# Layer 0's mixing half fed with x before its norm's row factor, in a two-layer hybrid decoder trunk

## The chip, the cores and the metric

The kernel runs on one core of one Trainium2 chip. The metric is the device time of one execution in microseconds (us), the median of several runs.

## The reference

Two layers, each a token-mixing half and an MLP half, over 256 tokens of 1024 channels. All arithmetic is float32.

```python
h = rmsnorm(x, ln_mix_pre[l])                 # x * rsqrt(mean(x^2) + eps) * gain
xr, yr, q, kv, g_nsa, qm, g_merge = split(h @ w_in[l])
o_a = rglru_branch(xr, yr, ...)               # conv, gates, scan, * gelu(yr)
o_b = nsa_branch(q, kv, g_nsa, positions, ...)  # rotary; compressed, selected, windowed
o_c = memory_branch(qm, mem, ln_mem[l], w_mem_kv[l])  # 4 heads into rmsnorm(mem)
merged = ga*(o_a @ w_br_rnn[l]) + gb*(o_b @ w_br_nsa[l]) + gc*(o_c @ w_br_mem[l])
x = x + rmsnorm(merged @ w_out[l], ln_mix_post[l])
x = x + rmsnorm(square(relu(rmsnorm(x, ln_mlp_pre[l]) @ mlp_w1[l])) @ mlp_w2[l], ln_mlp_post[l])
```

The row factor of a norm is one number per token, rsqrt(mean(x^2) + eps). A product h @ w is the row factor times (x * gain) @ w.

## The kernel before

Weights come from HBM in units of 128x1024 float32 (`raw`, five buffers, 512 KB each), and each unit is split into two fp32r parts: ScalarE (ACT) copies it to `whi`, and VectorE (DVE) writes the rest, `wlo` = raw - whi (`split_unit`; four buffers of each). Activations are split in the same way (`hTh` and `hTl` for layer 0's input, `hmh` and `hml` for the MLP's, `mTh` and `mTl` for the normed memory). Each product is then three matmuls: high by high, high by low, low by high. A unit is 24 matmuls of 256 columns or 12 of 512.

`ORDER0` and `ORDER1` list the jobs of each layer; `run` issues their units one after the other on TensorE (PE). In layer 0 the first job is `xr1`, the second `xr0`, then `yr0`, `yr1`, `vm0`, `km0`. All else (norms, evacuations of PSUM, scores, softmax, scans) are generators called lanes. A lane says on which engine its next piece runs, and `side`, called after each step of six or twelve matmuls, advances every lane whose next piece is due. What is due is decided by a clock per engine (`Order.T`), which `Meter` advances by a cost for every instruction as it is written; a PE piece of a lane is put in when its inputs are due at the PE's clock (`TOL` 0.07 us). So the costs in `Meter` set the order of the program, and all engines run that order as written. All instructions are recorded through line 140, so a row is told by its tiles.

The program's start: x comes as four tiles `xt[t][h]` (two of tokens by two of channels, 256 KB each). `first_norm` squares and sums them on ACT (`junk`), makes the row factor on GpSimd (POOL: `mean`, `var`, `rstd`), scales x on DVE (`hn`), and `quarter` transposes `hn` on PE (`tr`), four quarters of 256 channels, whose results are multiplied by the gain's column `gcol` as they are split. `warm` matmuls are filler, with no use of their result. The memory's norm (`mem_prep`, `mnorm`) loads six tiles (1.5 MB, gain and `mem`), squares on ACT, scales on DVE (`hn` again) and transposes on PE (`tr` again); its result is first used by `vm0`. At the end of a mixing half the residual and the MLP's norm follow in the same way (POOL `rstd`, DVE `hn`, PE `tr`).

Of the kernel before, what the change touches and what calls it, by code (L numbers as in the profile page):

```python
# [11 lines left out]
F32 = mybir.dt.float32  # L12
# [93 lines left out]
class Meter:  # L106
# [39 lines left out]
def trunk_kernel(ctx, tc, x, mem, positions, ln_mix_pre, w_in, conv_w, conv_b, lru_wr, lru_br, lru_wi, lru_bi,  # L146
# [269 lines left out]
    warm, gcol = [], []  # L416

# [16 lines left out]
    def first_norm(o):  # L434

        hn = {}

        def scale(t):
            yield "A"
            el, box = first_half(xt[t][0])  # L440
            s1 = half_sumsq(xt[t][1])
            yield el
            yield "G"
            r = rstd_of(box[0], s1)
            for h in range(2):
                yield "D"
                hn[t, h] = a([P, 512], F32, "hn")
                dve.tensor_scalar(hn[t, h], xt[t][h], r, None, op0=OP.mult)

        def quarter(q):  # L450
            while len(hn) < NT * 2 and not all((t, q // 2) in hn for t in range(NT)):
                yield scaled
# [21 lines left out]
        scaled = [spawn(scale(t), prio=0) for t in range(NT)]  # L474
        for q in range(4):
            spawn(quarter(q), f"first{q}", prio=0)

# [168 lines left out]
    def run(jobs):  # L646
# [83 lines left out]
    nsin = cp.tile([P, 3, 32], F32, name="nsin")  # L730
    per = a([P, 2, 64], F32, name="per")
# [13 lines left out]
    def rope_tables():  # L745
# [38 lines left out]
        dve.tensor_scalar(cos, h, -2.0, 1.0, op0=OP.mult, op1=OP.add)  # L784

    def rope_mul(src, nh, s, t1, t2, rows=P):

        r = slice(0, rows)
# [155 lines left out]
    def mem_score_lane(t, qm, km, pr):  # L944
# [12 lines left out]
        dve.tensor_scalar(mx, mx, -1.0 / 16, None, op0=OP.mult)  # L957
# [3 lines left out]
        for h in range(2):  # L961
            act.activation(p[:, h, :], sc[:, h, :], AF.Exp, scale=1.0 / 16, bias=mx[:, h:h + 1],
# [36 lines left out]
    def mem_lane(l, rnd, qm, km, vm, o):  # L999
        pr = {}  # L1000
        yield [spawn(mem_score_lane(t, qm, km, pr)) for t in range(NT)]
# [342 lines left out]
    def layer(l):  # L1344
# [4 lines left out]


        def xr_epi(half):
            def go(banks):
                E["xs", half] = [a([P, 2, S], F32, "xs") for _ in range(2)]
                yield "A"
                for b in range(2):
                    act.activation(E["xs", half][b], banks[b], AF.Copy)
# [3 lines left out]
        def yr_epi(half):  # L1360
            def go(banks):
                ys = [a([P, 2, S], F32, "ys") for _ in range(2)]
                yield "A"
                for b in range(2):
                    act.activation(ys[b], banks[b], AF.Copy)
# [55 lines left out]
        def g_done(half, i):  # L1421
            def lane(t, o):
                tg = E["tg", i, half, t] = a([P, 512], F32, "tg")
                yield "A"
                act.activation(tg, o, AF.Tanh, scale=0.5)
# [55 lines left out]
        def kc_epi(j, banks):  # L1481
            st = a([P, 2, S], F32, "kcs")
            yield "A"
            act.activation(st, banks[j], AF.Copy)
# [13 lines left out]
        def kv_epi(br):  # L1498
            def go(t, banks):
# [3 lines left out]
                for w in range(2):  # L1503
                    act.activation(vx[w][:, :, 0:3:2, :], dup(v[:, 2 * w:2 * w + 2], [P, 2, 2, 64]), AF.Copy)
                yield "D"
                t1, t2 = a([P, 256], F32, "rt1"), a([P, 256], F32, "rt2")
                rope_mul(banks[t][:, 0:256], 4, t, t1, t2)
                for w in range(2):
                    dve.tensor_tensor(vx[w][:, :, 1, :], v[:, 2 * w:2 * w + 2], f(vx[w][:, :, 0, :]), op=OP.subtract)
# [17 lines left out]
        def gn_job():  # L1527
# [11 lines left out]
            def lane():  # L1539
                th = a([48, S], F32, "gth")  # L1540
                yield "A"
                act.activation(th, st["b"], AF.Tanh, scale=0.5)
                free("mm")
# [14 lines left out]
        def q_epi(half):  # L1558
            def one(t, banks):
                t1, t2 = a([P, 512], F32, "rt1"), a([P, 512], F32, "rt2")  # L1560
                yield "D"
                rope_mul(banks[t], 8, t, t1, t2)
# [190 lines left out]
    def mem_prep(l):  # L1753
# [10 lines left out]
        od.cur.r = max(od.cur.r, dma_clock[0] + 2.0)  # L1764
        spawn(norm_both(ms, gm, env[l]["M"], f"mnorm{l}"))

    def load_x(t):
        for h in range(2):
# [5 lines left out]
    dma_clock[0] = 2.4 + 4 * 0.73  # L1774
# [16 lines left out]
    od.cur.r = 4.5  # L1791
    spawn(column, "gcol", prio=0)
    first_norm(env[0]["X"])
    first_pre = order[0].pre

    def start():
        first_pre()
        mem_prep(0)
# [7 lines left out]
    order[0].pre = start  # L1806
    od.cur.r = 0.0
    run(order)
# [31 lines left out]
```

## Time and profile before

| | before |
|---|---|
| median of the runs shown (1216.6 to 1221.95) | 1221.04 us |
| the profiled execution's own time | 1221.59 us |
| its span in the trace | 1219.9 us |
| PE busy | 1199.6 us of the span |
| DVE busy | 901.6 us |
| ACT busy | 736.7 us |

The span is the profiled execution from the first to the last instruction; 1.69 us of its own time lie outside. Busy time of PE is modelled with the latency of each matmul (283 ns for one of 256 columns that starts 120 ns after the one before), so short gaps don't show in it: gaps are read from the starts of matmuls in the timeline.

### The profile page before, as it was taken

The page shows a single profiled execution, that of the slowest core. Times are in us where ns is not written, and L with a number is a line of the kernel's source. Part 1 is how long each engine was busy: PE and PEld are TensorE (multiplying, and loading weights), DVE is VectorE, ACT ScalarE, POOL GpSimd, SP SyncE. Part 2 cuts the span into 40 slices and gives each one's busy share as a digit, 9 for nine tenths or more (in the row PEclk, how much of TensorE's full clock was granted, in tenths as well). Part 3 has the DMA queues.
Part 4 walks back from the last instruction along what each step waited for, and adds up shares of the span by engine and source line. Part 5 has one row for each costly group of instructions (what it writes and reads, how often), then busy time and mean ns, then how long its engine had stood idle before and what let it go on. Part 6 is the DMA issues. An engine that isn't in the chain of part 4 may idle for free.

```text
span 1219.9 us, 19570 instructions
## 1 busy us (share of the span) xinstructions
PE 1199.6 (98%) x7371; PEld 1068.8 (88%) x7371; DVE 901.6 (74%) x1516; ACT 736.7 (60%) x1330; POOL 35.5 (3%) x88
## 2 busy tenths in 40 slices
PE   8899999999999999999999999999999999999997
PEld 7899988888888889998989999888888887899896
DVE  4778897979898686555557587998978877655555
ACT  4677856777666465445456688675656655645443
POOL 3000000000000020000001000000000001000000
PEclk9899999999999999999999999999999999999999
DMA  8555656753345666666656556584534356565561
GB/s 283 181 161 168 190 156 181 223 152 108 122 131 186 233 191 191 194 189 189 206 174 210 154 171 176 153 258 140 154 121 138 121 164 217 166 187 183 190 190 69
DMA packets 121263, 212.58 MB, mean 174 GB/s; under 512 B 10441, under 2 KB 24098, under 8 KB 121169
## 3 DMA queue, kind: packets, MB, share of 16 engines
q1 hardware_dynamic: 120752, 211.19, 55.9%
q8 instruction: 58, 0.95, 0.3%
q0 software_dynamic: 416, 0.15, 0.1%
q14 instruction: 37, 0.30, 0.1%
HBM read 208.16 MB, written 1.05 MB: 172 GB/s over the span
## 4 chain that ended last, share of the span: by engine, by line
PE 92%; DVE 2%; DMA 2%; ACT 2%; issue 1%; SPq 0%; POOL 0%; POOLq 0%; DVEq 0%; ACTq 0%
PE mm L140 62%; PE acc L140 14%; PE ob L140 2%; PE sc L140 2%; PE wo L140 2%; PE pt L140 2%; PE hid L140 1%; PE gp L140 1%; PE mo L140 1%; PE msc L140 1%; PE tr L140 1%; DMA mem<-in_mem_dram 1%; ACT junk L140 1%; DVE wlo L140 1%; DMA raw<-in_mlp_w_dram 1%
## 5 line engine op out<-in xcount | busy, mean ns | idle before, releaser
L140 DVE TENSOR_TENSOR wlo<-raw,whi 128x1024 fp32r<-128x1024 f32 (+1 forms) x371 | 447.1, 1214 | 225.7 <-ACT whi L140 224.3
L140 ACT ACTIVATE whi<-raw 128x1024 fp32r<-128x1024 f32 (+1 forms) x371 | 385.3, 1055 | 204.9 <-PE mm L140 117.0
L140 PE MATMUL mm<-hmh,whi 128*128 128x256 f32 x480 | 135.9, 283 | 0.0
L140 PE MATMUL mm<-hmh,wlo 128*128 128x256 f32 x480 | 135.9, 283 | 0.0
L140 PE MATMUL mm<-hml,whi 128*128 128x256 f32 x480 | 135.9, 283 | 0.0
L140 PE MATMUL mm<-hTh,whi 128*128 128x256 f32 x448 | 129.4, 289 | 0.0
L140 PE MATMUL mm<-whi,hTh 128*128 128x512 f32 x320 | 129.1, 403 | 0.0
L140 PE MATMUL mm<-hTh,wlo 128*128 128x256 f32 x448 | 127.6, 285 | 0.0
L140 PE MATMUL mm<-hTl,whi 128*128 128x256 f32 x448 | 127.6, 285 | 0.0
L140 PE MATMUL mm<-wlo,hTh 128*128 128x512 f32 x320 | 125.1, 391 | 0.0
L140 PE MATMUL mm<-whi,hTl 128*128 128x512 f32 x320 | 125.0, 391 | 0.0
L140 PE MATMUL acc<-whi,rh 128*128 128x512 f32 x256 | 99.8, 390 | 0.0
L140 PE MATMUL acc<-wlo,rh 128*128 128x512 f32 x256 | 99.8, 390 | 0.0
L140 PE MATMUL acc<-whi,rl 128*128 128x512 f32 x256 | 99.6, 389 | 0.0
L140 PEld LDWEIGHTS mm<-hmh,whi 128*128 128x128 f32 x480 | 92.1, 192 | 0.5
L140 PEld LDWEIGHTS mm<-hml,whi 128*128 128x128 f32 x480 | 92.1, 192 | 0.5
L140 PEld LDWEIGHTS mm<-hmh,wlo 128*128 128x128 f32 x480 | 92.1, 192 | 0.0
L140 PEld LDWEIGHTS mm<-hTh,whi 128*128 128x128 f32 x448 | 86.9, 194 | 0.2
L140 PEld LDWEIGHTS mm<-hTl,whi 128*128 128x128 f32 x448 | 86.9, 194 | 0.2
L140 PEld LDWEIGHTS mm<-hTh,wlo 128*128 128x128 f32 x448 | 86.7, 194 | 0.0
L140 PEld LDWEIGHTS mm<-whi,hTl 128*128 128x128 f32 x320 | 60.1, 188 | 13.1
L140 PEld LDWEIGHTS mm<-whi,hTh 128*128 128x128 f32 x320 | 60.2, 188 | 12.0 <-issue 0.2
(311 smaller groups left out, 2467.7 us busy)
## 6 DMA issues: line engine op xcount, KB each, us to landing
raw<-in_w_in_dram SPq DMA_DIRECT2D x136, 512.0 KB, 3.7
raw<-in_mlp_w_dram SPq DMA_DIRECT2D x128, 512.0 KB, 4.2
raw<-in_w_mem_kv_dram SPq DMA_DIRECT2D x32, 512.0 KB, 4.2
raw<-in_cmp_w_dram SPq DMA_DIRECT2D x16, 512.0 KB, 4.0
raw<-in_w_br_rnn_dram SPq DMA_DIRECT2D x16, 512.0 KB, 3.7
raw<-in_w_br_mem_dram SPq DMA_DIRECT2D x16, 512.0 KB, 3.7
raw<-in_w_br_nsa_dram SPq DMA_DIRECT2D x16, 512.0 KB, 3.7
raw<-in_w_out_dram SPq DMA_DIRECT2D x16, 512.0 KB, 4.5
```

The source lines that it names most:

```text
L140: return fn(*args, **kw)
```

## The change

In layer 0's mixing half the matmuls take x times the gain, without the row factor. `quarter` transposes `xt` itself. The sums of squares, POOL's chain and the factor (`rfac`: times 1, 1/2, 1/16 and -1/16) come later, and the factor enters where a result leaves PSUM: as the scale of ACT's activation where tokens lie on partitions (merge gates, values, memory scores), in rotary tables made for layer 0 (`rot`: 6 small DVE instructions), and where tokens lie along a row, by multiplying with `rows`, the factor of all 256 tokens on every partition. `rows` is made on PE as ones times a diagonal matrix (`spread`, tile `rs`, two float32 matmuls) and copied by DVE. With `by_rows` ten 128x512 evacuations of layer 0 (4 `xs`, 4 `ys`, 2 `kcs`) move from ACT to DVE, and the branch gates' tile gets one DVE instruction more. The half of x with channels 512 to 1023 is loaded behind the first two weight units; the memory's loads and norm go from the first job to the second. In `Meter` the cost of an fp32r matmul of n columns goes from 0.0025 + n/2400 to 0.0133 + n/2400 us.

```diff
-                    cost = max(load, 0.0025 + n / 2400.0) * (4 if args[1].dtype == F32 else 1)
+                    cost = (max(load, 0.0133 + n / 2400.0) if args[1].dtype != F32 else 4 * max(load, 0.001 + n / 2400.0))
...
+    rows = cp.tile([P, S], F32, name="rows")
+    rfac = cp.tile([P, NT, 4], F32, name="rfac")
...
-    def first_norm(o):
+    def first_operands(o):
+        ones = a([P, P], F32, "ones")
+        pool.memset(ones, 1.0)
+        diag = {}
...
-                    pe.transpose(pt[:, i, t * P:(t + 1) * P], hn[t, q // 2][:, c * P:(c + 1) * P], ident)
+                    pe.transpose(pt[:, i, t * P:(t + 1) * P], xt[t][q // 2][:, c * P:(c + 1) * P], ident)
...
+        def scale(t):
+            yield "A"
+            el, box = first_half(xt[t][0])
+            s1 = half_sumsq(xt[t][1])
+            yield el
+            yield "G"
+            r = rstd_of(box[0], s1)
+            yield "D"
+            for i, c in enumerate((1.0, 0.5, 1.0 / 16, -1.0 / 16)):
+                dve.tensor_scalar(rfac[:, t, i:i + 1], r, c, None, op0=OP.mult)
+            diag[t] = a([P, P], F32, "diag")
+            dve.tensor_scalar(diag[t], ident, r, None, op0=OP.mult)
+        def spread():
+            yield [spawn(scale(t)) for t in range(NT)]
+            yield "M1"
+            pt = bank([P, NT, P], "mm", "rs")
+            for t in range(NT):
+                pe.matmul(pt[:, t, :], ones, diag[t], start=True, stop=True)
+            yield "D"
+            dve.tensor_copy(rows, pt.rearrange("p t c -> p (t c)"))
+            free("mm")
...
+    def by_rows(dst, src, shape):
+        dve.tensor_tensor(dst, src, bc(rows[:shape[0]], "p (o s) -> p o s", shape), op=OP.mult)
...
+            if nd == 2:
+                between()
...
+        def channel_copy(dst, banks):
+            if l == 0:
+                yield "@rows"
+                yield "D"
+                for b in range(2):
+                    by_rows(dst[b], banks[b], [P, 2, S])
...
-    def load_x(t):
-        for h in range(2):
+    def load_x(h):
+        dma_clock[0] += 2 * 0.73
+        for t in range(NT):
             nc.sync.dma_start(out=xt[t][h], in_=x[0, t * P:(t + 1) * P, 512 * h:512 * h + 512])
+    column = load_column(ln_mix_pre[0:1, :])
     load_x(0)
-    column = load_column(ln_mix_pre[0:1, :])
-    load_x(1)
...
     def start():
         first_pre()
-        mem_prep(0)
...
+    def second():
+        second_pre()
+        mem_prep(0)
...
+    order[0].pre, order[1].pre = start, second
+    order[2].pre = lambda: drain("rows")
+    order[11].pre = lambda: drain("const")
...
+    run(order, lambda: load_x(1))
```

How the order moves is shown at three places. The first is PE at the program's start, up to the first matmul of `xr1` (`hn` is scaled x, `xt` is x as loaded, 93 and 95 its first half of channels), before:

```order
L140 MATMUL warm_130<-dmask,identr 128x256 x16
L140 MATMUL gcol_147<-ident,grow_108 128x8
L140 MATMUL tr_183<-ident,hn_169 128x128 x2
L140 MATMUL tr_183<-ident,hn_179 128x128 x2
L140 MATMUL warm_130<-dmask,identr 128x256 x2
L140 MATMUL tr_192<-ident,hn_169 128x128 x2
L140 MATMUL tr_192<-ident,hn_179 128x128 x2
L140 MATMUL warm_130<-dmask,identr 128x256 x2
L140 MATMUL tr_199<-ident,hn_173 128x128 x2
L140 MATMUL tr_199<-ident,hn_181 128x128 x2
L140 MATMUL warm_130<-dmask,identr 128x256 x2
L140 MATMUL mm_263<-hTh_112,whi_208 128x256
```

and now:

```order
L140 MATMUL warm_136<-dmask,identr 128x256 x16
L140 MATMUL gcol_153<-ident,grow_108 128x8
L140 MATMUL tr_157<-ident,xt_93 128x128 x2
L140 MATMUL tr_157<-ident,xt_95 128x128 x2
L140 MATMUL warm_136<-dmask,identr 128x256 x2
L140 MATMUL tr_166<-ident,xt_93 128x128 x2
L140 MATMUL tr_166<-ident,xt_95 128x128 x2
L140 MATMUL warm_136<-dmask,identr 128x256 x2
L140 MATMUL mm_210<-hTh_114,whi_175 128x256
```

Three of the four quarters stood ahead of the first `mm`, and half of their transposes read tiles of either half of x; now two quarters stand ahead of it, both of the first half, and the other two follow after 12 matmuls.

The second is ACT from the splits of the fifth and sixth unit on (`junk` from `mem` is the memory's sum of squares, `xs` the evacuation of `xr1`), before:

```order
L140 ACTIVATE whi_344<-raw_128 128x1024
L140 ACTIVATE whi_374<-raw_214 128x1024
L140 ACTIVATE junk_392,ss_393<-mem_230 128x512
L140 ACTIVATE junk_395,ss_396<-mem_232 128x512
L140 ACTIVATE junk_398,ss_399<-mem_234 128x512
L140 ACTIVATE junk_401,ss_402<-mem_236 128x512
L140 ACTIVATE xs_416<-mm_263 128x512
L140 ACTIVATE xs_417<-mm_264 128x512
L140 ACTIVATE whi_426<-raw_220 128x1024
```

and now, later in the program (`whi_588` is the eleventh unit, `whi_680` the thirteenth):

```order
L140 ACTIVATE whi_588<-raw_368 128x1024
L140 ACTIVATE whi_645<-raw_403 128x1024
L140 ACTIVATE whi_680<-raw_464 128x1024
L140 ACTIVATE junk_700,ss_701<-mem_413 128x512
L140 ACTIVATE junk_703,ss_704<-mem_415 128x512
L140 ACTIVATE junk_706,ss_707<-mem_417 128x512
L140 ACTIVATE junk_709,ss_710<-mem_419 128x512
L140 ACTIVATE whi_734<-raw_530 128x1024
```

The memory's four sums stood behind the sixth unit's split and ahead of the seventh's; now they stand behind the thirteenth's and ahead of the fourteenth's, and `xs` is no longer on ACT.

The third is PE at the end of layer 0's mixing half, where the MLP's norm is transposed (`mm` is a unit of layer 1's `vm0`; `hn` the MLP's normed input, 5138 and 5140 or 5148 and 5150 the first 128 tokens), before:

```order
L140 MATMUL mm_5062<-whi_5088,mTh_4325 128x512
L140 MATMUL mm_5062<-wlo_5089,mTh_4325 128x512
L140 MATMUL mm_5062<-whi_5088,mTl_4326 128x512
L140 MATMUL mm_5063<-whi_5088,mTh_4325 128x512
L140 MATMUL mm_5063<-wlo_5089,mTh_4325 128x512
L140 MATMUL mm_5063<-whi_5088,mTl_4326 128x512
L140 MATMUL tr_5178<-ident,hn_5138 128x128 x4
L140 MATMUL tr_5183<-ident,hn_5140 128x128 x4
L140 MATMUL tr_5188<-ident,hn_5152 128x128 x4
L140 MATMUL tr_5193<-ident,hn_5154 128x128 x4
L140 MATMUL mm_5222<-mTh_4319,whi_5120 128x256
L140 MATMUL mm_5222<-mTl_4320,whi_5120 128x256
```

and now:

```order
L140 MATMUL mm_5082<-whi_5075,mTl_4429 128x512
L140 MATMUL tr_5178<-ident,hn_5148 128x128 x4
L140 MATMUL tr_5183<-ident,hn_5150 128x128 x4
L140 MATMUL mm_5081<-whi_5110,mTh_4430 128x512
L140 MATMUL mm_5081<-wlo_5111,mTh_4430 128x512
L140 MATMUL mm_5081<-whi_5110,mTl_4431 128x512
L140 MATMUL mm_5082<-whi_5110,mTh_4430 128x512
L140 MATMUL mm_5082<-wlo_5111,mTh_4430 128x512
L140 MATMUL mm_5082<-whi_5110,mTl_4431 128x512
L140 MATMUL tr_5208<-ident,hn_5168 128x128 x4
L140 MATMUL tr_5213<-ident,hn_5170 128x128 x4
```

The first eight transposes stand 12 matmuls of 512 columns further ahead in the stream, the other eight 6 matmuls. At the end of layer 1's mixing half the eight transposes of the first tokens stand 3 matmuls of 512 columns further ahead. In both layers' attention the lanes' pieces stand earlier among the job matmuls too, by up to about a hundred matmuls of 512 columns near the end of layer 1's attention, as part of the same reordering.

## Rows read from the trace of the kernel before

**Rows 1.** The page, parts 1 and 5: busy time and share; one group of VectorE.
```profile
PE 1199.6 (98%) x7371; PEld 1068.8 (88%) x7371; DVE 901.6 (74%) x1516; ACT 736.7 (60%) x1330; POOL 35.5 (3%) x88
...
L140 DVE TENSOR_TENSOR wlo<-raw,whi 128x1024 fp32r<-128x1024 f32 (+1 forms) x371 | 447.1, 1214 | 225.7 <-ACT whi L140 224.3
```

**Rows 2.** Waits of PE, whole span: us in total, times, longest us.
```profile
PE tr L140 <- DVE hn L140: 9.2, 5, 3.2
PE gn L140 <- DVE wlo L140: 0.9, 1, 0.9
```

**Rows 3.** Windows: stretch, busy us (instructions) by engine, PEclk, DMA share, GB/s.
```profile
0.00:13.60 13.60, 7.78 (x35) 7.23 (x36) 4.21 (x11) 6.69 (x14) 8.08 (x28) 0.87 0.81 270
...
10.10:13.40 3.30, 3.15 (x15) 3.16 (x16) 2.04 (x6) 2.43 (x5) 3.30 (x7) 0.50 0.98 364
...
17.20:31.40 14.20, 14.20 (x120) 14.20 (x120) 4.96 (x5) 6.28 (x13) 1.83 (x6) 1.00 0.96 321
...
31.40:41.00 9.60, 6.44 (x33) 6.24 (x32) 7.73 (x18) 4.91 (x10) 0.59 (x2) 0.64 0.61 182
```

**Rows 4.** Timeline, 5 to 17 us: start us, us, engine, what, [idle before, releaser].
```profile
5.38 0.63 ACT L140 ACTIVATE junk<-xt 128x512 bf16<-128x512 f32 x1 [0.54 <-DMA xt<-in_x_dram]
...
6.20 0.27 PE L140 MATMUL gcol<-ident,grow 8*128 8x8 f32 x1
...
7.96 0.63 ACT L140 ACTIVATE junk<-xt 128x512 bf16<-128x512 f32 x1 [1.85 <-DMA xt<-in_x_dram]
...
10.25 0.69 PE L140 MATMUL tr<-ident,hn 128*128 128x128 f32 x2 [2.67 <-DVE hn L140]
...
10.97 0.84 ACT L140 ACTIVATE hTh<-tr,gcol 128x256 fp32r<-128x256 f32 x2 [2.29 <-PE tr L140]
...
12.64 2.42 DVE L140 TENSOR_TENSOR wlo<-raw,whi 128x512 fp32r<-128x512 f32 x3
...
13.61 0.28 PE L140 MATMUL mm<-hTh,whi 128*128 128x256 f32 x1
...
17.15 0.28 PE L140 MATMUL mm<-hTh,whi 128*128 128x256 f32 x1
```

**Rows 5.** Timeline, 28 to 41 us.
```profile
28.34 0.63 ACT L140 ACTIVATE junk<-mem 128x512 bf16<-128x512 f32 x1 [7.17 <-DMA mem<-in_mem_dram]
...
31.53 0.28 PE L140 MATMUL mm<-hTh,wlo 128*128 128x256 f32 x1
...
34.97 1.12 PE L140 MATMUL tr<-ident,hn 128*128 128x128 f32 x4 [3.16 <-DVE hn L140]
...
36.10 0.41 PE L140 MATMUL mm<-hTl,whi 128*128 128x256 f32 x1
...
36.31 0.41 PE L140 MATMUL mm<-hTh,wlo 128*128 128x256 f32 x1
...
40.78 0.28 PE L140 MATMUL mm<-hTl,whi 128*128 128x256 f32 x1
```

**Rows 6.** Timeline of PE, 75 to 77 us.
```profile
75.09 1.02 PE L140 MATMUL gp<-xc,gw 128*128 128x256 f32 x4
...
76.18 0.40 PE L140 MATMUL mm<-wlo,mTh 128*128 128x512 f32 x1
```

**Rows 7.** Timeline, 440 to 446 us.
```profile
440.73 0.57 POOL L140 TENSOR_TENSOR rstd<-var,mhalf 128x1 f32<-128x1 f32 x1
...
443.23 0.96 POOL L140 TENSOR_TENSOR rstd<-var,mhalf 128x1 f32<-128x1 f32 x1
...
444.23 1.41 DVE L140 SCALAR_TENSOR_TENSOR hn<-xt,rstd,gain 128x512 f32<-128x512 f32 x2 [0.46 <-POOL rstd L140]
...
444.38 0.39 PE L140 MATMUL mm<-whi,mTl 128*128 128x512 f32 x1
...
444.61 1.91 PE L140 MATMUL tr<-ident,hn 128*128 128x128 f32 x16
```

**Rows 8.** Timeline of PE at 1029 us.
```profile
1028.71 1.32 PE L140 MATMUL tr<-ident,hn 128*128 128x128 f32 x8 [1.64 <-DVE hn L140]
```

More of the change, by code (lines that the diff above doesn't have):

```diff
@@ L472, in quarter @@
             free()
-        scaled = [spawn(scale(t), prio=0) for t in range(NT)]
+        def scale(t):
[19 more added lines that the diff above has]
+            free("mm")
         for q in range(4):
+            od.cur.r = 5.0 if q < 2 else 10.2
             spawn(quarter(q), f"first{q}", prio=0)
+        od.cur.r = 16.0
+        spawn(spread(), "rows", prio=0.2, child=0.2)
+    def by_rows(dst, src, shape):
+        dve.tensor_tensor(dst, src, bc(rows[:shape[0]], "p (o s) -> p o s", shape), op=OP.mult)
     def busy(n):
@@ L644, in weave, with run @@
         return Job([js[n].units[i] for _, n, i in turns], lambda: None, mm, unit_need=unit_need)
-    def run(jobs):
+    def run(jobs, between):
         us, flat = [], []
@@ L730, in trunk_kernel @@
     nsin = cp.tile([P, 3, 32], F32, name="nsin")
+    rot = (cos, sin, nsin)
     per = a([P, 2, 64], F32, name="per")
@@ L784, in rope_tables, with rope_mul @@
         dve.tensor_scalar(cos, h, -2.0, 1.0, op0=OP.mult, op1=OP.add)
-    def rope_mul(src, nh, s, t1, t2, rows=P):
+        yield "@rows"
+        yield "D"
+        tabs = a([P, 3, NT, 32], F32, "rot")
+        for i, v in enumerate(rot):
+            for t in range(NT):
+                dve.tensor_scalar(tabs[:, i, t, :], v[:, t, :], rfac[:, t, 0:1], None, op0=OP.mult)
+        env[0]["rot"] = [tabs[:, i] for i in range(3)]
+    def rope_mul(src, nh, s, t1, t2, rows=P, tab=None):
+        cos, sin, nsin = tab or rot
         r = slice(0, rows)
@@ L1000, in mem_lane @@
         pr = {}
-        yield [spawn(mem_score_lane(t, qm, km, pr)) for t in range(NT)]
+        yield [spawn(mem_score_lane(l, t, qm, km, pr)) for t in range(NT)]
         yield [spawn(mem_out_lane(h, pr, vm, o.hi[2 * rnd + h], o.lo[2 * rnd + h]), f"memo{l}{2 * rnd + h}")
@@ L1348, in layer @@
         win = w_in[l]
+        def channel_copy(dst, banks):
+            if l == 0:
+                yield "@rows"
+                yield "D"
+                for b in range(2):
+                    by_rows(dst[b], banks[b], [P, 2, S])
+            else:
+                yield "A"
+                for b in range(2):
+                    act.activation(dst[b], banks[b], AF.Copy)
         def xr_epi(half):
@@ L1353, in go @@
                 E["xs", half] = [a([P, 2, S], F32, "xs") for _ in range(2)]
-                yield "A"
-                for b in range(2):
-                    act.activation(E["xs", half][b], banks[b], AF.Copy)
+                yield from channel_copy(E["xs", half], banks)
                 free("mm", 2)
@@ L1362, in go @@
                 ys = [a([P, 2, S], F32, "ys") for _ in range(2)]
-                yield "A"
-                for b in range(2):
-                    act.activation(ys[b], banks[b], AF.Copy)
+                yield from channel_copy(ys, banks)
                 free("mm", 2)
@@ L1424, in lane @@
                 yield "A"
-                act.activation(tg, o, AF.Tanh, scale=0.5)
+                act.activation(tg, o, AF.Tanh, scale=rfac[:, t, 1:2] if l == 0 else 0.5)
                 free("mm")
@@ L1540, in lane @@
                 th = a([48, S], F32, "gth")
+                if l == 0:
+                    yield "D"
+                    dve.tensor_tensor(th, st["b"], rows[:48], op=OP.mult)
+                    free("mm")
                 yield "A"
-                act.activation(th, st["b"], AF.Tanh, scale=0.5)
-                free("mm")
+                act.activation(th, st["b"] if l else th, AF.Tanh, scale=0.5)
+                if l:
+                    free("mm")
                 yield "P1"
@@ L1561, in one @@
                 yield "D"
-                rope_mul(banks[t], 8, t, t1, t2)
+                rope_mul(banks[t], 8, t, t1, t2, tab=E.get("rot"))
                 free("mm")
@@ L1804, in start @@
         spawn(const_lane(), "const")
-    order[0].pre = start
+    second_pre = order[1].pre
+    def second():
[4 more added lines that the diff above has]
+    order[11].pre = lambda: drain("const")
     od.cur.r = 0.0
-    run(order)
+    run(order, lambda: load_x(1))
 _INS = ["x", "mem", "positions", "ln_mix_pre", "w_in", "conv_w", "conv_b", "lru_wr", "lru_br", "lru_wi", "lru_bi",
```

49 lines of the change are left out of this document (23 added, 26 removed).

## The prediction

> **What bounds the kernel now.** I read the page first. PE is busy 98% of the span, DVE 74%, ACT 60% [rows 1]: where PE runs without a gap, no other engine's saving counts, and what PE is given more to do counts in full. The list of PE's waits came next: `tr` for `hn` costs 9.2 us in five waits, the longest 3.2, and the largest of the attention's is one 0.9 us wait of `gn` [rows 2]. Windows then tell the stretches apart [rows 3]. From 17.2 to 31.4 PE starts 120 matmuls in 14.2 us, 0.118 each: nothing to win. From 31.4 to 41.0 it starts 33 in 9.6 us, at a mean granted clock of 0.64. And before 13.6 it has done nothing that counts. So two stretches hold recoverable time, and the timeline shows what each waits for.
>
> At the start, x's second pair of tiles lands so that ACT squares the last one at 7.96; POOL and DVE follow, the transposes start at 10.25, `hTh` at 10.97, and the first job matmul stands behind all four quarters, at 13.61. The second unit's first matmul starts at 17.15 [rows 4].
>
> In the second stretch ACT stands 7.17 us at 28.34, waiting for `mem`'s transfer. Its queue is in order, so the seventh unit's split, `xs` and the memory's norm come after; PE first runs out of split weights and then waits 3.16 us for `hn` before the memory's transposes at 34.97 [rows 5]. After that wait two neighbours start 0.21 apart, 36.10 and 36.31, where 0.118 was usual: the clock's lower level, 1.2 GHz.
>
> **The change part by part**, against the profiled execution's own 1221.59 us, 0.55 above the median of the runs.
>
> *A, the start.* The first two quarters need the first two x tiles and `gcol`. ACT began on a third tile at 5.38, so the first two have landed, and they now stand ahead of the rest; `gcol` ran at 6.20 [rows 4]. So q0's transposes start at about 6.4, q1's follow, and `hTh` starts at 7.1. From `hTh` (10.97) to the end of the first of three `wlo` halves (12.64 + 2.42/3 = 13.45) took 2.5 us, so `wlo` is there at 9.6, if the weights are. They are: four x tiles, 1 MB, had landed by 7.96, and two x tiles with the first unit are the same 1 MB. Two matmuls can run on `whi` alone; ten more at 0.118 reach 10.8; q2's and q3's eight transposes at 0.11 and four `warm` take 1.35, to 12.15; twelve matmuls take 1.4. The second unit starts at 13.55 where it started at 17.15: **-3.6**. The second half of x and ACT's splits of the second unit lie beside this.
>
> That is at the full clock. From 10.1 to 13.4 the granted clock was 0.50 [rows 3], after PE had stood 2.67 us before 10.25 [rows 4]; the new start has a shorter pause, some 1.6 us from q1's end at 8.0 to 9.6, and I take the full clock.
>
> The Trainium skill's page "TensorE: Matmul & The Clock Gate", section "Part 1: The HAM clock gate", says that the throttled state is the default and that activity releases it, the moment shifting from run to run. The rows agree as to the two levels; by that rule the first stretch could stay at the lower one, and A would be worth the smaller sum that the first rival gives.
>
> *B, `rs`.* Two float32 matmuls of 128 columns that PE did not have. Two of 256 (`gp`, four records) hold PE from 75.09 to 76.18, 1.09 us [rows 6]; half the columns, half of it: **+0.5**, and 1.1 at most if a float32 matmul's price is not in its columns; not under 0.2, what two fp32r matmuls would take.
>
> *C, the second stretch.* From the start at 31.53 to that at 40.78 lie 20 matmuls and eight transposes, 20 x 0.118 + 8 x 0.11 = 3.25 us of work in 9.25 [rows 5]: **-6.0**. The memory's loads now go behind the second job's gate load and its sums stand behind ACT's thirteenth split instead of the sixth. With four `whi` buffers that split waits for the ninth unit's end, 13.55 + 8 x 24 x 0.118 = 36.2. Up to the last `mem` tile SP's queue now holds some 10 MB, at 321 to 364 GB/s, as in two windows [rows 3], 27 to 31 us: I estimate the tiles landed at 30 to 34, two to six us ahead. Without it ACT would stand again. The least this can be worth is the transposes' wait alone, -3.2.
>
> *D, end of layer 0's mixing half.* The first eight transposes stand 12 matmuls earlier, at 0.23 (444.38 to 444.61): PE reaches them at 441.85 instead of 444.61 [rows 7]. The first tokens' `rstd` is ready at 441.30; one split fewer stands ahead of `hn` on DVE, whose two halves (1.41 together) would end at about 442.1 and 442.8: two waits of 0.2 and 0.25. The second tokens' `rstd` ends at 444.19 and their `hn` at 444.94 and 445.64; PE, after six matmuls, is there at about 444.5: waits of 0.45 and 0.2. **+1.1**; nothing at the least, if POOL is quicker, 2.8 at most, all that was moved.
>
> *E, end of layer 1's.* The first transposes already wait 1.64 us [rows 8], and three matmuls that stood ahead of them now stand behind: 3 x 0.23, **+0.7**.
>
> *F, the lanes' places.* The new cost is 0.120 for 256 columns and 0.227 for 512, which is what PE takes (0.118 and 0.23); the old one was 0.109 and 0.216. With PE's clock as `Meter` keeps it no longer ahead of the real one, pieces go in earlier among the matmuls and with less slack. I take **+0.6**, less than one wait like `gn`'s; the bounds are -0.9, `gn`'s wait gone, and +3, three waits of that kind.
>
> *At no cost:* ten evacuations on DVE instead of ACT (about 0.61 each, half a `wlo` of 1.214 [rows 1]), the `rot`, `rfac`, `diag` and `rows` steps, and the scales, which ride in instructions that were there. DVE's spare quarter and PE's full stream cover them; uncovered they are some 6 us. ACT, which splits weights, gets lighter.
>
> Sum: -3.6 + 0.5 - 6.0 + 1.1 + 0.7 + 0.6 = -6.7, so 1214.9 of own time, and 1214.3 against the median, taking off the 0.55.
>
> **The rivals.**
>
> *The start stays at the lower clock, or the weights land late.* Twelve matmuls, eight transposes and twelve matmuls from 10.0 to 13.5 would take nearly as long again where they run at 1.2 GHz: +1.6 with half of them caught, 3.5 with all. 1215.9 to 1217.8. For: the clock fell in this very stretch before. Against: the wait of 1.64 us [rows 8] is as long as the new pause, and PE keeps `warm` filler between the quarters.
>
> *Lane pieces that PE waits for, the side on which it gets slower.* In the two layers' attention stand 48 groups of `pt` transposes among the matmuls, now put in just when due by a model. If each comes before its softmax is done, PE stops 48 times. A wait of 6.7/48 = 0.14 us each eats the gain; from 0.27 it is slower by more than 0.5%; 0.3, a third of `gn`'s wait, gives 1228.7. For: DVE is the busiest engine beside PE and takes over ten evacuations, so its real times may run behind the model's. Against: a piece goes in only after a step of six matmuls, which leaves on average half a step, 0.7 us, and before, one wait of this kind showed in two layers.
>
> *The row factor comes late.* `rs` stands in PE's order after the first job's units, at 13.55 + 3 x 24 x 0.118 = 22.0, and everything behind it waits if `diag` isn't there. ACT's squares now follow its fourth split, from about 15.3 on, four of 0.8 with the read of the sum; POOL's three steps for the second token tile follow at 18.5, 0.57 each if they are quick; `diag` is there near 20.5. But one and the same `rstd` took 0.57 and 0.96 [rows 7]. If each POOL step stood behind a `wlo` of 1.2 us, three cost up to 3.7, 1.9 more than counted, 0.4 past the slack of 1.5; if all six of the two tiles do, 3.8 more: 1214.7 to 1216.6.
>
> The Trainium skill's page "SBUF — State Buffer", section "Who interferes with whom", has a DVE instruction with two inputs in SBUF, as `wlo` is, contend with a GpSimd instruction that reads SBUF. The 0.96 beside 0.57 agrees; by that rule this rival is as likely as splits are dense there.
>
> *The change does not remove the wait for `mem`.* If the loads land at 39 or later, ACT stands again and C shrinks to nothing: 1220.3.
>
> *More than forecast:* the earlier pieces also take `gn`'s 0.9 and half of D and E: 1212.5.
>
> **How the numbers follow.** Chances: the forecast 0.45, lower clock 0.2, lane waits 0.15 (two thirds of them under 0.27 each), row factor 0.07, the wait for `mem` 0.05, more than forecast 0.08. The range 1210.0 to 1219.5 leaves out lane waits beyond 0.11 each, the wait for `mem`, and a gain in which B, D and E cost nothing and F gives its most. A measurement of this kernel can tell about 0.5% from no change; that bound lies at 1214.9, half a microsecond above the forecast, so the bounds of B, D and F alone throw it to either side: faster 0.47, same 0.45, and slower, for the worst third of lane waits and a bad DVE, 0.08.
>
> **What would show it.** Right: the first job matmul at 9 to 9.6 and the second unit at 13.5; granted clock near 1.00 from 10 on; the memory's `junk` without an idle time by DMA; no gap in PE from 31 to 41, and no wait of `rs` at 22; `tr` waits of about 1 us in sum at layer 0's boundary and about 2.3 at layer 1's. Wrong: a granted clock of 0.5 after 10 (first rival); a list of PE's waits in which `pt`, `ob` or `gn` for DVE or ACT come many times (second); `rs` waiting for `diag` (third); a long wait of ACT for `mem` at any later place. If the early transposes at the boundaries wait more than 2.8 us, D was mis-sized by what sits on POOL and DVE ahead of `hn`.

## The result, and the profile after

The changed kernel takes 1238.5 us (1237.19 to 1238.75), the kernel before 1217.54 in five runs (1215.06 to 1221.95): 21 us more. The estimate of the ratio from all runs is 1.0158, interval 1.0132 to 1.0183 (the two medians alone give 1.017). It is slower, where the prediction had 1214.3 and at most 1219.5. The profiled execution took 1238.75, its span is 1237.0.

The page and PE's list of waits, of the changed kernel (us in total, times, longest):

```profile
PE 1208.3 (98%) x7375; PEld 1072.3 (87%) x7375; DVE 913.7 (74%) x1553; ACT 729.6 (59%) x1308; POOL 40.4 (3%) x89
...
PE mm L140 <- DVE wlo L140: 7.3, 6, 3.7
PE mm L140 <- DVE rt L140: 4.2, 2, 3.9
PE tr L140 <- DVE hn L140: 3.5, 4, 1.7
...
PE pt L140 <- DVE pl L140: 1.2, 1, 1.2
```

PE is as busy as before by the page, 98%. What changed is the kind of wait: `tr` for `hn`, 9.2 us in [rows 2] and 5.5 in a second trace of the kernel before that comes below, is down to 3.5, and the job matmuls themselves, which waited for almost nothing, now wait 7.3 us for split weights and 4.2 for a PSUM bank that a rotary evacuation (`rt`) still reads.

The windows of [rows 3], of the changed kernel (busy us and instructions by engine, then PE's clock):

```profile
0.00:13.60 13.60, 9.76 (x60) 8.71 (x61) 4.95 (x10) 6.75 (x14) 9.41 (x29) 1.00 0.82 265
10.10:13.40 3.30, 3.28 (x27) 2.87 (x26) 2.20 (x4) 2.88 (x7) 2.64 (x5) 1.00 1.06 366
17.20:31.40 14.20, 14.20 (x120) 14.19 (x120) 11.52 (x40) 7.05 (x11) 1.69 (x5) 1.00 1.02 313
31.40:41.00 9.60, 9.60 (x82) 9.60 (x81) 9.12 (x28) 5.04 (x10) 0.71 (x2) 1.00 0.89 307
```

The first 41 us are much as forecast: full clock throughout, 82 matmuls in the stretch that had 33. The loss comes later. The timeline of its two largest stops, of the changed kernel:

```profile
217.53 1.35 DVE L140 TENSOR_TENSOR rt<-mm,rot 128x512 f32<-128x512 f32 x3
219.52 2.35 DVE L140 TENSOR_TENSOR wlo<-raw,whi 128x1024 fp32r<-128x1024 f32 x2
221.79 0.21 DVE L140 TENSOR_TENSOR t<-kcp,cos 64x64 f32<-64x64 f32 x1
222.37 1.34 DVE L140 TENSOR_TENSOR rt<-mm,rot 128x512 f32<-128x512 f32 x3
223.86 0.76 PE L140 MATMUL mm<-whi,hTh 128*128 128x512 f32 x1 [3.90 <-DVE rt L140]
224.42 0.63 PE L140 MATMUL mm<-wlo,hTh 128*128 128x512 f32 x1
...
759.66 0.36 DVE L140 TENSOR_TENSOR gs<-g,pet 128x120 f32<-128x120 f32 x1 [2.23 <-DMA g<-kcs]
760.68 0.88 DVE L140 TENSOR_TENSOR gs<-g,pet 128x120 f32<-128x120 f32 x3 [0.66 <-DMA g<-kcs]
762.62 0.88 DVE L140 TENSOR_TENSOR gs<-g,pet 128x120 f32<-128x120 f32 x3 [0.68 <-DMA g<-kcs]
763.41 1.22 DVE L140 TENSOR_TENSOR wlo<-raw,whi 128x1024 fp32r<-128x1024 f32 x1
764.68 0.58 PE L140 MATMUL mm<-hTh,wlo 128*128 128x256 f32 x1 [3.74 <-DVE wlo L140]
```

In layer 0 DVE evacuates q's first token tile at 217.53, then writes two splits, then the compression's `t`, and only at 222.37 the second tile, whose bank PE needs: PE stands 3.90 us, and the next matmuls start 0.43 to 0.56 apart, where 0.23 is usual. In layer 1 DVE stands for the compression's gather (`gs` from `g`, 2.23, 0.66 and 0.68 us), the split comes behind it, and PE waits 3.74 us for that. Windows over these places, below, show a mean clock of 0.65 and 0.58, so the matmuls behind a stop cost time too: set against the same matmuls in the second trace of the kernel before, they fall 3.1 us further behind from 223.86 to 231.46 and 2.4 from 764.68 to 769.97. The Trainium skill's page "TensorE: Matmul & The Clock Gate", section "Part 1: The HAM clock gate", calls the throttled state the default that activity releases; these rows agree.

```profile
217.50:232.00 14.50, 9.85 (x35) 7.53 (x36) 11.90 (x23) 5.53 (x9) 0.00 (x0) 0.65 0.43 125
764.00:772.00 8.00, 7.32 (x31) 6.87 (x32) 7.97 (x17) 7.13 (x12) 0.00 (x0) 0.58 0.56 160
```

### The profile page after: what moved, and what is told of

Same layout as the page of the kernel before. It is cut to its first block, busy times and chain, and to the rows that moved or that the text cites. A ratio compares the mean times of both kernels' runs of the same rounds, so it can differ in the third digit from the quotient of the medians.

```text
span 1237.0 us, 19620 instructions
## 1 busy us (share of the span) xinstructions
PE 1208.3 (98%) x7375; PEld 1072.3 (87%) x7375; DVE 913.7 (74%) x1553; ACT 729.6 (59%) x1308; POOL 40.4 (3%) x89
## 4 chain that ended last, share of the span: by engine, by line
PE 85%; DVE 6%; ACT 4%; issue 2%; DMA 1%; POOL 1%; SPq 1%; DVEq 0%; POOLq 0%; ACTq 0%
PE mm L140 57%; PE acc L140 14%; PE ob L140 2%; PE sc L140 2%; DVE wlo L140 2%; PE wo L140 2%; PE pt L140 2%; PE mo L140 1%; ACT whi L140 1%; PE hid L140 1%; PE tr L140 1%; PE msc L140 1%; ACT junk L140 1%; DVE xc L140 1%; PE gp L140 1%
## 5 line engine op out<-in xcount | busy, mean ns | idle before, releaser
L140 ACT ACTIVATE pr<-sc,mx 128x256 f32<-128x256 f32 (+1 forms) x128 | 52.0, 427 | 36.7 <-DVE mx L140 35.6
```

## The experiments

The kernels ran against the kernel before, whose median was 1217.5 to 1219.2 from job to job. These medians differ by 1.7 us, so a smaller difference between runs of different jobs says nothing. Lags given below are differences between the starts of one and the same job matmul in two traces, read where the same lane pieces lie behind both. The names of the runs stand in brackets.

**What the first 41 us were worth.** The memory's part of the change alone (`e4_only_mem`):

```diff
+    order[0].pre, order[1].pre = start, second   # second: second_pre(), mem_prep(0)
-        od.cur.r = max(od.cur.r, dma_clock[0] + 2.0)
+        od.cur.r = max(od.cur.r, dma_clock[0] + (2.0 if l else 12.0))
```

> The kernel before with the memory's loads and norm in the second job in place of the first, and no other part of the change. If ACT's wait for these transfers cost the 6.0 us that the prediction put down to it: about 1211.5, with no gap of PE between 31 and 41. If other work takes the wait's place, or the shifted places of the lanes cost as much: 1216 to 1219.

The time is 1218.81, ratio 1.0003 (0.9994 to 1.0013). The gap between 31 and 41 is gone (83 matmuls in 31.4 to 41.0), and yet the time is that of before. So the kernel before ran again for a second trace, with no edit:

> The kernel before once more, for a second trace. Its 13 later runs have a median of 1217.8, 3.8 below the profiled one, and moving the memory's norm alone gave 1218.8. If the profiled run of before owed that to the low clock from 33.9 to 40.8 (6.8 us at half rate, up to 3.4 us lost): this trace is near 1218 with a granted clock near 1.00 from 34 to 41 and the same waits. If not: the same clock and about 1221.

One run, 1215.8. Its windows and timeline:

```profile
10.10:13.40 3.30, 3.30 (x22) 3.30 (x22) 3.04 (x5) 3.30 (x8) 2.56 (x5) 1.00 0.91 331
17.20:31.40 14.20, 13.24 (x111) 13.04 (x110) 5.61 (x7) 7.36 (x14) 1.97 (x6) 1.00 0.89 307
31.40:41.00 9.60, 9.60 (x83) 9.60 (x84) 8.98 (x29) 7.39 (x15) 0.00 (x0) 1.00 0.75 222
...
6.28 0.63 ACT L140 ACTIVATE junk<-xt 128x512 bf16<-128x512 f32 x1
...
8.76 0.69 PE L140 MATMUL tr<-ident,hn 128*128 128x128 f32 x2 [0.93 <-DVE hn L140]
...
24.63 0.63 ACT L140 ACTIVATE junk<-mem 128x512 bf16<-128x512 f32 x1 [4.95 <-DMA mem<-in_mem_dram]
...
31.28 0.66 PE L140 MATMUL tr<-ident,hn 128*128 128x128 f32 x4 [0.96 <-DVE hn L140]
```

This execution of the same kernel squares x's last tile at 6.28 instead of 7.96 [rows 4], transposes at 8.76 instead of 10.25, keeps the full clock, and waits 0.96 us for the memory's `hn` instead of 3.16 [rows 5]. Its span is 1214.1 against 1219.9. The two executions stand near the two ends of the kernel's runs (1215.36 to 1223.28, median 1217.75), and a good part of what the prediction read as the kernel's recoverable time was that of one execution: here the stretch from 17.2 to 31.4 lacks 9 matmuls (111 for 120), 1.1 us, and that from 31.4 to 41.0 lacks none. In the run with the memory's part alone these 1.1 us are won and two waits at 84 us, 0.58 and 0.76, take them back (its own start, which the edit leaves as it was, is the latest of all traces, 14.21 for the first job matmul, where the two of the kernel before have 13.61 and 12.12):

```profile
84.38 0.39 PE L140 MATMUL mm<-mTh,whi 128*128 128x256 f32 x1 [0.58 <-ACT whi L140]
85.64 0.39 PE L140 MATMUL mm<-mTh,wlo 128*128 128x256 f32 x1 [0.76 <-DVE wlo L140]
```

**The planner's cost, and the evacuations.** The new cost alone, on the kernel before (`e2_only_cost`):

```diff
-                    cost = max(load, 0.0025 + n / 2400.0) * (4 if args[1].dtype == F32 else 1)
+                    cost = (max(load, 0.0133 + n / 2400.0) if args[1].dtype != F32 else 4 * max(load, 0.001 + n / 2400.0))
```

> The kernel before with the new matmul cost in the planner and nothing else. Theory (the cost does the harm): 13 to 25 us slower than before, 1231 to 1242, with the same four places in the list of gaps. Rival (evacuations on DVE do it): within 3 us of before, 1215 to 1221.

1240.37, ratio 1.0190 (1.0172 to 1.0209): one line of the planner, which adds no instruction, is worth the whole loss. It does more than reorder. Some pieces go on ACT or DVE as `Meter`'s clocks say, and here 17 small ones (14 `pr`, 2 `ct`, 1 `r`) move from ACT to DVE and two `mp` the other way, DVE busy 906.7 us for 901.6. The line also lowers the cost of float32 matmuls by 0.006 us; that part stays in every run with the old cost behind the start, and two of them, below, stand at 1216.5 and 1219.7. The opposite, the changed kernel with the old cost behind the start (`e1_old_cost_late`):

```diff
-                    cost = (max(load, 0.0133 + n / 2400.0) if ...
+                        cost = max(load, (0.0025 if order.T["P"] > 50.0 else 0.0133) + n / 2400.0)
```

> The changed kernel, with the old matmul cost (0.0025 + n/2400) in the planner from its 50th microsecond on, the new one before. In the trace of the changed kernel PE is 9 us ahead of before at 50 us, and loses 26 us by the end in four places (3.5 at 128, 9 at 217 to 227, 6.5 at 765, 2 at 890, small ones) where splits of weights stand on DVE and ACT behind lane pieces that wait. Theory (the new cost put those pieces too early): the places go, 9 us stay won, about 1209. Rival (the evacuations moved to DVE delay the splits, whatever the cost): 1225 to 1238.

1232.25, ratio 1.0123 (1.0106 to 1.0140). The theory as put would have had 1209. The stops at 765 and 891 are gone, but layer 0 has new ones, at 199 and 393:

```profile
PE pt L143 <- DVE pr L143: 3.8, 2, 2.1
PE mm L143 <- DVE vx L143: 2.9, 1, 2.9
...
198.80 0.47 PE L143 MATMUL mm<-whi,hTh 128*128 128x512 f32 x1 [2.89 <-DVE vx L143]
```

To this kernel, the ten evacuations given back to ACT (`f2_act_evac_old_cost`; the row factor is left out there):

```diff
-                yield "D"
+                yield "A"
-                    by_rows(dst[b], banks[b], [P, 2, S])
+                    act.activation(dst[b], banks[b], AF.Copy)      # and kcs likewise
```

> The changed kernel with the old cost from the planner's 50th microsecond on (1232.3 as measured), and the ten evacuations xs, ys and kcs of layer 0 on ACT again, without the row factor, which is left out there. If the ten evacuations on DVE cause layer 0's losses of 16 us at 199 and 393 under the old cost: about 1212 to 1217. If it is the changed order in general: 1225 to 1235, with stops at other places.

1216.52, ratio 0.9987 (0.9974 to 1.0000): the 16 us are gone. Against the second trace of the kernel before it is 1.7 us ahead at 209 and 1.3 behind at 220, by a wait of 1.3 us for `rt` and what follows it. Work or plan? In `g2_dve_evac_act_order` DVE does the ten multiplications, but the planner counts them on ACT, so that every other instruction keeps its place (on every engine the two traces have the same sequence but for these ten):

```diff
+    def by_rows_as_act(dst, src):
+        nc.vector.tensor_tensor(dst, src, bc(rows, "p (o s) -> p o s", [P, 2, S]), op=OP.mult)
+        od.note("A", 0.055 + 512 / 1200.0, dst.tensor.name, [src.tensor.name])
...
-                    act.activation(dst[b], banks[b], AF.Copy)
+                    by_rows_as_act(dst[b], banks[b])             # and kcs likewise
```

> The ten evacuations multiply by the row factor on DVE as in the changed kernel, but the planner counts them as ACT's, with the old cost from its 50th microsecond on: the order of every other instruction on every engine is then that of the run with ACT's evacuations (1216.5). The only difference to the run at 1232.3 is the order that the planner makes of it. If the work of ten evacuations on DVE is what costs 16 us: 1225 to 1233. If it is the order that the planner makes when it counts them on DVE: 1215.5 to 1219.

1219.73, ratio 1.0010 (0.9997 to 1.0022). The work costs about the 3.2 us between this and the run before it, of which the trace shows 1.25 in one wait, of PE for a split behind an evacuation (57.97). The other 12.5 us up to 1232.25 are the plan, which is the order and the choice of engine together. The fourth cell, new cost with ACT's evacuations (`f5_act_evac_new_cost`, the edit of `f2_act_evac_old_cost` without its cost line):

> The changed kernel with its new cost throughout and the ten evacuations of layer 0 on ACT, without the row factor, which is left out there: the fourth cell beside 1216.5 (old cost, ACT), 1232.3 (old cost, DVE) and 1238.5 (new cost, DVE). If the two harms add: 1222 to 1225. If either alone spoils layer 0's order and the new cost layer 1's: 1232 to 1242, with layer 1's losses of about 10 us from 700 to 900 as in the changed kernel.

1237.67, ratio 1.0154 (1.0136 to 1.0171), with the stops of the changed kernel. Under the new cost it makes 0.8 us of difference where the evacuations are done, which is no more than the jobs differ.

**Layer by layer.** From the run at 1219.73, the new cost in layer 1 alone (`h3_new_cost_l1`) and in layer 0's mixing half alone (`h4_new_cost_l0`):

```diff
-0.0025 if order.T["P"] > 50.0 else 0.0133
+0.0025 if 50.0 < order.T["P"] < 640.0 else 0.0133     # h3
+0.0133 if order.T["P"] < 430.0 else 0.0025            # h4
```

> The run whose evacuations go on DVE in ACT's places (1219.7), with the new cost in the planner's time behind 640 us, in layer 1 alone. If the new cost harms layer 1 by itself: 1229 to 1231, with the stops at 765, 890 and 928 of the changed kernel, 10 us in all. If layer 1's losses came from what layer 0's plan handed on: 1219 to 1222.

> The same run with the new cost up to the planner's 430 us, in layer 0's mixing half alone. If it harms layer 0 by itself: 1229 to 1231, with the stop at 217 to 227. If the harm needs evacuations planned on DVE: 1219 to 1222.

1229.18 (ratio 1.0091, 1.0075 to 1.0107) and 1229.44 (1.0089, 1.0071 to 1.0107): 9.5 and 9.7 more than 1219.73. Added to it they give 1238.9, the changed kernel's 1238.5. The two layers lose apart from each other. In layer 0 it is the order and hardly the choice of engine: four `pr` go to DVE and one `ct` leaves it, DVE busy 911.6 us for 911.3.

In layer 1 the same 40 us of job matmuls (counted at 0.227 and 0.118 each from the program's start) lie between 711.9 and 759.7 of the run at 1219.73 and between 712.3 and 769.3 of the run with the new cost in layer 1:

```profile
711.90:759.70 47.80, 47.80 (x357) 45.95 (x356) 39.08 (x69) 37.65 (x63) 0.00 (x0) 1.00 0.64 182
712.30:769.30 57.00, 53.25 (x381) 51.15 (x380) 47.69 (x83) 41.41 (x68) 0.00 (x0) 0.94 0.57 164
```

In the second there are 24 more lane pieces on PE (381 for 357, memory scores `msc`), 14 more DVE instructions and 8.6 us more DVE work (47.69 for 39.08) beside the same jobs: the plan has moved lane work ahead, and PE's clock is 0.94. Of the 9.2 us of difference some 2.8 are these 24 pieces, at 0.118 each, which are missing later; the rest is one stop, of 3.75 us at 753.25 for a split, and the matmuls at the lower clock behind it.

**By which way the cost harms.** Six edits, each with an idea of the cause. The compression's gather planned later, in the changed kernel (`e3_late_gather`) and in the run with the new cost in layer 1 alone (`h5_new_cost_l1_late_gather`):

```diff
-            od.cur.r += 3.0
+            od.cur.r += 8.0                       # h5: 8.0 if l else 3.0
             yield spawn(blocks_lane(l, j, g2, E["gx"]), prio=0.5)
```

> The changed kernel; the pieces that read the compression's gathered tiles (gs from g) are planned 8 us behind the evacuation in place of 3. In the changed kernel DVE stood for their transfers 6.3 us in seven waits, just ahead of PE's stops at 128 and 765. If those waits are the cause at these two places: about 3.5 + 6.4 us less, 1228 to 1230, and the stops at 217 to 227 and 890 stay. If the splits are late for another reason there: 1236 to 1239.

> The run with the new cost in layer 1 alone, and layer 1's pieces that read the compression's gathered tiles planned 8 us behind the evacuation in place of 3. If DVE's wait for the gather is the cause of the stop at 765 and of the low clock behind it: 4 to 6.5 us less than the run with the new cost in layer 1 alone, 1223 to 1226. If the splits are late there for another reason: the same as that run within 2 us.

1235.44 (1.0150, 1.0132 to 1.0168) and 1227.68 (1.0076, 1.0060 to 1.0092): 3.1 and 1.5 us won, not 10 and 5. The stop at 765 goes in both. In the second the 24 pieces and DVE's extra work go with it: the jobs that took 57.0 us take 49.5, with 41.75 us of DVE's. What was won is lost again at other places: waits for splits of 1.1 us at most each between 759 and 810, and in the second `tr` for `hn` at the end of the layer waits 2.94 us at 1032.64, for 1.77. Both rotary evacuations of q in one piece in layer 0 (`h1_rope_together`):

```diff
+                yield "D"
+                for t in range(NT):
+                    rope_mul(banks[t], 8, t, *tt[t], tab=E.get("rot"))
+                free("mm", 2)
```

> The changed kernel; in layer 0 the two token tiles' rotary evacuations of q go on DVE as one piece, so that no split and no compression step stands between them. If layer 0's stop at 223.9 (4.1 us and the low clock behind it, 9.4 in all) is the second tile's PSUM bank, held by what stands ahead of its evacuation: 1228 to 1231 against 1238.5. If the order ahead of it is at fault: 1236 to 1242, with a stop at the same place.

1239.25 (1.0168, 1.0150 to 1.0186). The stop moves from 223.86 to 219.52 and is shorter, 2.12 us. The lag to the changed kernel is -3.2 at 237, and back to -0.1 at 394, by waits of 0.77 us at most:

```profile
216.13 1.23 DVE L140 TENSOR_TENSOR wlo<-raw,whi 128x1024 fp32r<-128x1024 f32 x1 [2.77 <-ACT whi L140]
219.52 0.47 PE L140 MATMUL mm<-whi,hTh 128*128 128x512 f32 x1 [2.12 <-DVE rt L140]
```

The split ahead of it waited 2.77 us for ACT, which has a step of the compression's chain and `kh` ahead: the time is that of the second theory, the order ahead of the evacuation. Three settings of the planner, all on the new cost: lane pieces only 1 us after they are due (`f3_tol_minus1`), ACT's and DVE's costs up by 9%, the ratio to PE of the old cost (`f4_scaled_act_dve`), and, in the run with the new cost in layer 1, ACT and DVE not planned more than 1 us ahead of PE (`i1_new_cost_l1_horizon`):

```diff
-                            if r > now + TOL:
+                            if r > now + (TOL if now < 50.0 else -1.0):                  # f3, DVE and ACT likewise
+            if key in "AD" and order.T["P"] > 50.0: cost *= 1.09                          # f4
-                        ... or od.T[e] > now + HORIZON:
+                        ... or od.T[e] > now + (HORIZON if now < 640.0 else 1.0):         # i1
```

> The changed kernel with the planner's tolerance at -1.0 us in place of 0.07 from its 50th microsecond on: a lane's piece goes in only 1 us after it is due. If the new cost does harm because pieces now stand with no slack: most of the 26 us lost after 50 us comes back, 1215 to 1225. If slack at the pieces is not what is missing (splits queue behind pieces wherever these stand): 1232 to 1245.

> The changed kernel with its new matmul cost, and the planner's costs of ACT and DVE raised by 9% from its 50th microsecond on, the same ratio to PE as under the old cost. If the old cost worked because it left ACT and DVE a tenth of headroom for each matmul: layer 1's 10 us come back and the time falls to 1226 to 1233, what the old cost gave, or below. If the ratio is not what matters: 1236 to 1245.

> The run with the new cost in layer 1 alone (1229.2), where from 640 us on a lane's piece goes on ACT or DVE only while that engine's planned clock is at most 1 us ahead of PE's, in place of 3. If the harm is that DVE's work is pulled forward, 47.7 us of it beside matmuls that had 39.1: 1219 to 1224. If each plan finds its own stops: 1226 to 1240, with the stops elsewhere.

1247.44 (1.0240, 1.0220 to 1.0260), 1246.15 (1.0216, 1.0196 to 1.0236) and 1233.52 (1.0130, 1.0107 to 1.0153). All three are worse than what they start from, but that alone clears none of the three ideas. With ACT's and DVE's costs up by 9% the changed kernel's stops shrink: PE's longest wait between 200 and 390 us is 0.76, the one at 765 is 0.74, and the lag to the changed kernel is -9.1 at 231 and -8.3 at 822. It is -0.4 at 403 and +6.9 at 1015: near the end of each layer's attention the lanes now come late, and PE waits for them, 2.50, 0.68 and 1.08 us from 394 to 403 and more in layer 1:

```profile
200.00:300.00 100.00, 98.92 (x551) 82.47 (x550) 81.36 (x170) 70.97 (x157) 0.00 (x0) 1.00 0.52 154
985.00:1016.00 31.00, 22.42 (x104) 18.56 (x105) 18.05 (x44) 14.69 (x36) 0.00 (x0) 0.72 0.15 46
...
987.03 0.58 PE L142 MATMUL ob<-pl,vx 128*128 128x256 f32 x1 [3.11 <-DVE pl L142]
1005.58 3.04 PE L142 MATMUL pt<-ident,pr 128*128 128x128 f32 x13 [3.43 <-DVE pr L142]
```

With the pieces 1 us later it is alike in layer 0 (lag -3.0 at 250, +11.4 at 415, where `pt` waits 2.93 us), and that edit also moves 100 `pr` from DVE to ACT. So in these traces the plan that pulls lanes ahead has its splits late, and the plans that hold lanes back have the attention's end late. That the planner's weighing of the engines turns the first kind into the second is read from these runs; no run at the new cost is without both. The third edit did not do what it was for: beside the same job matmuls (713.1 to 769.3) PE still has 380 instructions and DVE 46.4 us of work. Whether DVE's lead is the cause stays open.

**How much a small change of the plan costs.** Half a nanosecond more per matmul in the kernel before (`f1_cost_0030`), 0.0050 in the changed kernel behind its start (`g1_cost_0050`), and half a nanosecond less in the run at 1219.73 (`i2_act_order_0020`):

```diff
-0.0025
+0.0030        # f1; g1: 0.0050; i2: 0.0020
```

> The kernel before with 0.0030 in place of 0.0025 in the planner's matmul cost: half a nanosecond per matmul, of no meaning in itself, but lanes' pieces change places here and there. Theory (the new cost takes the pieces' slack, in proportion to the cost): under 1 us slower, 1217 to 1220. Rival (any other order than the one of before costs its share, since the one of before has no gaps): 5 to 15 us slower, 1223 to 1233.

> The changed kernel with a matmul cost of 0.0050 + n/2400 in the planner from its 50th microsecond on, between 0.0025 (1232.3) and 0.0133 (1238.5). If the losses of layer 0 with evacuations planned on DVE belong to any such plan: 1231 to 1238, with stops near 199 and 393. If they are those of one unlucky order: anywhere from 1218 to 1240, with stops at other places.

> The run whose evacuations go on DVE in ACT's places (1219.7), with 0.0020 in place of 0.0025 in the planner's matmul cost from its 50th microsecond on. By the theory that only the plan's luck differs at such small changes: within 1215 to 1224; it beats the kernel before if it comes under 1215, for which nothing speaks.

1219.72 (1.0012, 0.9997 to 1.0027), 1223.01 (1.0032, 1.0021 to 1.0044) and 1220.97 (1.0019, 1.0009 to 1.0029). At 0.0050 the changed kernel is 9 us faster than at 0.0025, so between these the time does not grow with the cost: the stop at 199 stays (2.89 us at 197.50), the two at 393 are gone. In the run with 0.0030 one wait at 394 (`mm` for `obl`, 1.6 us) and the clock behind it cost 4.2 us of lag, which other places give back in part. No version here beats the kernel before.

## Why the prediction was wrong, step by step

- **What bounds the kernel.** PE's busy share and the list of waits were read rightly, but the two stretches with recoverable time were those of one execution, 5.8 us of span longer than the second one, and the lag between the two, -5.8, is all there at 40 us. The text noted that the profiled time stood 0.55 above the median of three runs; over later runs it stands 4 above, and the second trace 2 below.
- **A** holds in its mechanism: first job matmul at 9.02 (forecast 9 to 9.6), full clock. The second unit starts at 14.26, not 13.55, since q2's and q3's transposes took until 12.82, not 12.15. Against [rows 4] that is -2.9, against the second trace of before, 15.66, it is -1.4, for -3.6. In the five traces with the start of before (one of them planned at the new cost) the second unit starts between 15.66 and 18.31, in the fifteen with the new start between 13.96 and 14.80: the new start is not only earlier but steadier. The first rival did not come.
- **B**: `rs` holds PE from 22.89 to 23.26, 0.37 for the 0.5 forecast, and did not wait; the row factor rival is out.
- **C**: the mechanism is right (no ACT wait for `mem`, no gap), the size was that execution's: 1.1 us against the second trace, not 6.0. At 80 us the changed kernel is 1.9 us ahead of the second trace of before, A, B and C together, where the sum had 9.1.
- **D**: 0.8 by the lag at 450, for 1.1. **E**: `tr` waits 1.74 and 1.17 us, where before it waited 1.64 [rows 8] and 1.06, and 1.88 and 1.09 in the second trace: 0.2 at most, for 0.7.
- **F is the step that failed.** It had +0.6, with +3 as the far bound, since the new cost is nearer to PE's real pace. The runs with the new cost in one layer show 9.5 and 9.7 us, and on the kernel before it costs 22. So F was off by some 18 us, most of the 24 between 1214.3 and 1238.5; the rest is mainly A and C, read from one execution. The step priced the plan by how well its clock matches, and bounded it by waits that the plan of before had left; neither says anything on the stops of another plan. The rival of the slower side had the right cause, the lanes' places, but looked at `pt`, which waits 1.2 us once; PE stops for its own job matmuls, a few times and long, and the lower clock behind the two longest adds 2.4 to 3.1 us to each.
- **The slower side's chance**, 0.08, was too small for the same reason: it rested on the waits in the trace of before, and 0.15 was all that the lanes' places had.
- **At no cost**: right in the main for the work of the evacuations (about 3.2 us). Not seen was that counting them on DVE makes another plan, 12.5 us under the old cost, 0.8 under the new.

The lag to the second trace of before goes from -1.9 at 80 us to +22.9 at the end: 4.1 up to 171 (most of it at the stop at 128.12, 1.93 us for a split), 9.5 from 187 to 240, 6.6 at 765, 1.7 from 875 to 1005, the rest in pieces under 1.

Shown is that the planner's cost line alone does it, that the two layers lose apart, and which instructions PE waits for. Open is why plans under this cost have such stops again and again (all eleven kernels that kept it in layer 0, in layer 1 or in both were 9 us or more slower than before) while those at 0.0020 to 0.0050 stood between 1.2 faster and 14.4 slower: six edits after one cause, tried singly, won 3.1 us at most, though some took away the very stops they were made for.

## What to carry to other kernels

Where a table of costs sets the order of four engines, a change of it is a new program, and a more exact cost is no evidence for a better one, nor does it stay a matter of order where the planner also picks engines; time it by itself before anything rides on it. When an edit moves work to another engine, run it once in the old order: that parts the price of the work (3 us here) from that of the plan (12). A variant that ends slower may still have mended the place it was made for: look where in the trace it gains and where it loses before its theory is dropped. And before a stretch of one profile is counted as recoverable, look at a second execution: where a profiled time lies at the top of the runs' spread, some of its gaps may be its own.

## Not expected of the hardware

Two executions of one program differed by 5.8 us, all of it before 40 us, where tiles landed late. In the slower one x's last tile was squared at 7.96, not 6.28, and the first job matmul started 1.5 us later; the first tile of `mem` was squared at 28.34, not 24.63, and the lag grew to 4.1 us at the memory's transposes; the last 1.7 came from matmuls at the lower clock (mean 0.64 from 31.4 to 41.0, and 0.50 already from 10.1 to 13.4; 1.00 in the other). Whether the first late tile made the second late is not shown.

And POOL's `rstd`, one instruction on 128 numbers, took 0.57 to 1.44 us in the changed kernel's boundary, 0.57 at 446.46, while DVE stood, and 1.44 at 448.61, beside a `wlo`:

```profile
446.46 0.57 POOL L140 TENSOR_TENSOR rstd<-var,mhalf 128x1 f32<-128x1 f32 x1
...
447.06 1.41 DVE L140 SCALAR_TENSOR_TENSOR hn<-xt,rstd,gain 128x512 f32<-128x512 f32 x2 [0.73 <-POOL rstd L140]
448.40 1.22 DVE L140 TENSOR_TENSOR wlo<-raw,whi 128x1024 fp32r<-128x1024 f32 x1
448.61 1.44 POOL L140 TENSOR_TENSOR rstd<-var,mhalf 128x1 f32<-128x1 f32 x1
```

The Trainium skill's page "SBUF — State Buffer", section "Who interferes with whom", has a DVE instruction with two inputs in SBUF contend with a GpSimd instruction that reads SBUF. The two rows agree with it; no run here parts it from another cause.
